# Passes of two gate/up units put side by side, transposes in groups of six and eight, a down unit in 256-column passes

## The chip, the cores and the metric

The kernel runs on one core of a Trainium2 chip. The metric is the device time of one execution in microseconds (us), as the median of several runs. TensorE (PE in the profile) multiplies; its weight loads are listed apart as PEld. VectorE is DVE, ScalarE is ACT, GpSimd is POOL, and SP issues most of the DMAs.

## What is computed

Two layers of a decoder trunk on 256 tokens with model width 1024. The parts that matter here:

```python
for l in range(DEPTH):                                # DEPTH = 2
    x = x + 0.5 * swiglu(rms_norm(x, ffn1_norm[l]), ffn1_gate[l], ffn1_up[l], ffn1_down[l])
    h = rms_norm(x, mix_norm[l]) @ w_in[l]
    # columns of h: pooling | q, k, v of block attention | q, k, v of dilated attention | convolution
    mix = jnp.concatenate([y_pool, y_moba, y_dil, y_conv], axis=-1)
    x = x + mix @ w_out[l]
    x = x + 0.5 * swiglu(rms_norm(x, ffn2_norm[l]), ffn2_gate[l], ffn2_up[l], ffn2_down[l])
return rms_norm(x, final_norm)
# swiglu(x, wg, wu, wd) = (silu(x @ wg) * (x @ wu)) @ wd ; hidden width 2816
```

All weights are float32 in HBM, and each is read once.

## The kernel before

**Weights.** All weights come as units of up to 128 x 2048 columns in a fixed order: for each FFN 22 gate/up units and 16 half down units (two for each of 8 output chunks), for each mixing stage 9 units of w_in and 4 of w_out. A unit lands in two halves (`raw`, four buffers). ACT writes its rounded part `hi` (type fp32r), DVE the rest `lo = raw - hi`; both lie in rings of five units. For three units per mixing stage (the last of w_in, the first two of w_out) ACT writes `lo = -hi` instead and a DMA of POOL adds the raw weights.

**Products.** Activations are split in the same way (`y_f`, `y_m`, `h`, `mx`: hi and lo side by side, 2 x 256 columns). A product is the sum of hi weights times both halves (one pass of 512 columns) and lo weights times the hi half (256 columns). `halves` (line 635) records all 512-column matmuls of a unit, then all 256-column ones, and the other way round at its next call. A gate/up unit has 16 of each, a half down unit 11 of each.

**FFN.** `ffn` (line 688) takes the 22 gate/up units one at a time (the first three of the first FFN together). Each writes two PSUM banks (`mm_gu`); ACT and DVE add up the halves (`t`), scale, apply SiLU and split the result into `h`. Then come the 8 down chunks (`dn`): each is added to `x` by two 256-column DVE operations, and `after(m)` starts the next norm's work on this chunk.

**Mixing stage** (`mix`, line 734). cg and ca (convolution input), then qkd and v (dilated attention), qkm (block attention), pu (pooling), then the output projection wo in the order of `W_OUT`: dilated, pooling, block attention, convolution. Beside these fp32r matmuls stand plain fp32 ones. `rope` (line 812) rotates q and k of each token half and turns them with four 128 x 128 transposes each (`tr_q`, `tr_k`). `scores` gives qk_d and qk_m; `softmax` gives p. `pv` (line 876) turns each head's p with three transposes (`pt`), copies them (`pts`, ACT) and multiplies with v. qk, pv and psw are small matmuls on 64 rows or 64 columns of the array, two at a time. The convolution is a chain of DVE operations on `yv`; then ACT adds the bias to `yv`, and its layer norm (line 936) takes the mean on PE (`ln`, with mean_w), squares (`lsq`), and sums them on PE (`ln` with ones).

**Order.** `Plan.order` (line 169) sets the order of all instructions beforehand: it keeps a clock for each engine, knows a cost for every operation and the buffers that it needs, and gives each engine the ready operation with the earliest due time. PSUM has eight banks: `mm` 0 to 3, `qk` 4 to 6, `sm` 7; gate/up and down units take the oldest of the first seven.

## Time and profile before

| | us |
|---|---|
| median of 3 runs | 936.9 (936.84 to 937.72) |
| profiled execution, device time | 935.79 |
| its span, first to last instruction | 934.0 |
| PE busy | 923.0 |
| DVE busy | 710.9 |
| ACT busy | 573.1 |

The time is that of the whole execution; the span is what the trace covers. A busy PE is a PE with a matmul under way, and matmuls overlap, so the length of a stretch of matmuls is read from the start of the first to the start of what follows, or from the chain of waits, which gives stretches of one kind end to end.

### The profile page before, as it was taken

The numbers are of one execution on the slowest core, as the hardware profiler recorded it, in microseconds if no ns is written. First come the engines' busy times: TensorE is split into PE (matmuls) and PEld (weight loads), VectorE is DVE, ScalarE is ACT, GpSimd is POOL, SyncE is SP. The second block draws the span as 40 slices with busy tenths as digits, with TensorE's granted clock in tenths as the row PEclk, the third lists the DMA queues.
The fourth block names the chain that finished last, engine by engine and source line by source line (L and its number), as shares of the span: only waits on it lengthen the run. The fifth ranks groups of instructions, "written<-read, shape, count | busy, mean of one in ns | idle before, by whom it ended". The sixth has DMA issues, their size and how long they took to land.

```text
span 934.0 us, 14720 instructions
## 1 busy us (share of the span) xinstructions
PE 923.0 (99%) x5460; PEld 813.1 (87%) x5460; DVE 710.9 (76%) x1323; ACT 573.1 (61%) x1055; POOL 44.3 (5%) x57
## 2 busy tenths in 40 slices
PE   9999999999999999999999999999999999999996
PEld 7888888887898888888888888888878988888885
DVE  7899965677978988766778887667698898876652
ACT  7776655558967655554646665445599675665540
POOL 0000000100102000000000000011010200000010
PEclk9999999999999999999999999999999999999998
DMA  8867456662965655456755554567557576554641
GB/s 300 283 215 244 149 155 195 234 217 85 257 207 180 211 195 185 125 177 190 255 199 181 190 187 139 164 193 252 184 125 207 168 249 215 195 168 125 186 125 46
DMA packets 56937, 176.45 MB, mean 189 GB/s; under 512 B 6560, under 2 KB 8608, under 8 KB 56864
## 3 DMA queue, kind: packets, MB, share of 16 engines
q1 hardware_dynamic: 54704, 168.92, 56.0%
q0 software_dynamic: 1728, 6.29, 3.5%
q8 instruction: 43, 0.70, 0.3%
q10 hardware_dynamic: 432, 0.29, 0.1%
q14 instruction: 30, 0.25, 0.1%
HBM read 174.43 MB, written 1.05 MB: 188 GB/s over the span
## 4 chain that ended last, share of the span: by engine, by line
PE 93%; DMA 2%; ACT 2%; DVE 1%; issue 0%; DVEq 0%; SPq 0%; ACTq 0%
PE mm_gu L370 52%; PE dn L370 26%; PE wo L370 3%; PE qkd L370 2%; PE v L370 1%; PE mm_cg L370 1%; PE pu L370 1%; PE mm_ca L370 1%; PE qkm L370 1%; DMA raw<-in_wo_dram 1%; DMA raw<-in_gu_dram 1%; ACT hi L311 1%; DMA x<-in_x_dram 1%; DVE lo L311 0%; PE qk_m L382 0%
## 5 line engine op out<-in xcount | busy, mean ns | idle before, releaser
L311 DVE TENSOR_TENSOR lo<-raw,hi 128x1024 fp32r<-128x1024 f32 (+3 forms) x353 | 374.0, 1083 | 68.5 <-ACT hi L311 52.0
L311 ACT ACTIVATE hi<-raw 128x1024 fp32r<-128x1024 f32 (+3 forms) x365 | 330.8, 939 | 141.9 <-PE dn L370 56.8
L370 PE MATMUL mm_gu<-y_f,hi 128*128 128x512 f32 x1408 | 331.9, 391 | 0.8 <-DVE y_f L348 0.4
L370 PEld LDWEIGHTS mm_gu<-y_f,hi 128*128 128x128 f32 x1408 | 260.5, 188 | 54.4 <-ACT hi L311 1.8
L370 PEld LDWEIGHTS mm_gu<-y_f,lo 128*128 128x128 f32 x1408 | 176.1, 192 | 4.2
L370 PE MATMUL mm_gu<-y_f,lo 128*128 128x256 f32 x1408 | 178.3, 283 | 0.0
L370 PE MATMUL dn<-h,hi 128*128 128x512 f32 x704 | 169.5, 391 | 0.0
L370 PEld LDWEIGHTS dn<-h,hi 128*128 128x128 f32 x704 | 128.8, 188 | 24.0
L311 DVE TENSOR_TENSOR t<-mm_gu,t 128x256 f32<-128x256 f32 x176 | 73.4, 421 | 52.0 <-ACT t L311 48.4
L370 PEld LDWEIGHTS dn<-h,lo 128*128 128x128 f32 x704 | 91.5, 191 | 4.3
L370 PE MATMUL dn<-h,lo 128*128 128x256 f32 x704 | 92.8, 283 | 0.0
L311 ACT ACTIVATE t<-mm_gu 128x256 f32<-128x256 f32 x176 | 64.6, 376 | 37.7 <-PE mm_gu L370 37.6
L311 ACT ACTIVATE h<-th 128x256 fp32r<-128x256 f32 x88 | 36.4, 417 | 63.1 <-DVE th L311 62.9
L311 DVE TENSOR_TENSOR t<-t,rb_f 128x512 f32<-128x512 f32 x88 | 60.2, 687 | 0.9
L311 ACT ACTIVATE th<-t 128x256 f32<-128x256 f32 x88 | 36.2, 414 | 34.9 <-DVE t L311 26.5
L348 DVE SCALAR_TENSOR_TENSOR x<-dn,x 128x256 f32<-128x256 f32 x64 | 27.0, 422 | 38.5 <-PE dn L370 37.9
L370 PE MATMUL wo<-mx,hi 128*128 128x256 f32 x256 | 47.6, 287 | 0.0
L348 DVE SCALAR_TENSOR_TENSOR yv<-hpad,par,yv 128x256 f32<-128x256 f32 x108 | 43.7, 475 | 0.0
L311 DVE TENSOR_TENSOR h<-th,h 128x256 fp32r<-128x256 f32 x88 | 36.9, 420 | 7.8 <-ACT h L311 6.8
L370 PEld LDWEIGHTS wo<-mx,hi 128*128 128x128 f32 x256 | 39.8, 192 | 0.7 <-issue 0.7
L311 DVE TENSOR_TENSOR th<-th,t 128x256 f32<-128x256 f32 x88 | 36.8, 419 | 2.4 <-ACT th L311 1.7
L370 PE MATMUL wo<-mx,lo 128*128 128x256 f32 x128 | 36.2, 283 | 0.0
(198 smaller groups left out, 651.7 us busy)
## 6 DMA issues: line engine op xcount, KB each, us to landing
raw<-in_gu_dram SPq DMA_DIRECT2D x170, 512.0 KB, 4.5
raw<-in_dn_dram SPq DMA_DIRECT2D x64, 384.0 KB, 3.6
raw<-in_dn_dram SPq DMA_DIRECT2D x64, 320.0 KB, 2.9
raw<-in_wi_dram SPq DMA_DIRECT2D x36, 512.0 KB, 4.8
raw<-in_wo_dram SPq DMA_DIRECT2D x16, 512.0 KB, 8.5
lo<-in_wo_dram POOLq DMA_DIRECT2D x8, 512.0 KB, 12.6
raw<-in_gu_dram SPq DMA_DIRECT2D x9, 256.0 KB, 5.7
lo<-in_wi_dram POOLq DMA_DIRECT2D x4, 512.0 KB, 9.4
```

The lines of the kernel that those rows point to most:

```text
L311: f(*[val(x) for x in a], **{n: val(x) for n, x in k.items()})
L348: nc.vector.scalar_tensor_tensor(out, in0=a, scalar=scalar, in1=b, op0=op0, op1=op1)
L370: nc.tensor.matmul(val(o), lhsT=val(lhsT), rhs=val(rhs), start=self.i == 0, stop=self.i == self.n - 1, skip_group_check=True)
```

## The change

Six edits.

- **Pairs.** From the first unit after the norm's row is known (unit 3 in most FFNs, unit 8 in the first one), gate/up units are taken two at a time: all 512-column passes of both, then all 256-column passes of both, and the reverse in the next pair. An odd last unit stays single.
- **Transposes.** `transposes` issues several at once. `rope` turns both token halves together (8 transposes), `pv` two heads together (6).
- **PSUM.** The first of the two pv banks of the dilated attention comes from the `mm` group.
- **Layer norm of the convolution.** One squaring of 512 columns and one addition of 256 columns on DVE, then two sums on PE in place of four.
- **Last down unit.** For the last chunk of the last FFN the first half's two additions to `x` come before the second half, which goes to a bank of its own in 33 passes of 256 columns; one addition follows it.
- **Planner.** A step on PE from fp32 to fp32r or back is charged `TURN` = 0.065; the costs of ACT and of DVE's tensor_tensor per column are raised by 5% and 3%.

```diff
+TURN = 0.065
+        o.kind = any(v.buf.dt == F32R for v in r)
-        out = []
+        out, kind = [], True
-            free[e] = now + o.cost
-            o.done = now + o.cost + o.lat
+            cost = o.cost
+            if e == "pe" and o.kind != kind:
+                cost += TURN
+                kind = o.kind
+            free[e] = now + cost
+            o.done = now + cost + o.lat
...
-        rec("act", 0.093 + 0.000833 * n + 0.093 * extra, nc.scalar.activation, w, [in_, k.get("scale"), k.get("bias")],
+        rec("act", 0.093 + 0.000875 * n + 0.093 * extra, nc.scalar.activation, w, [in_, k.get("scale"), k.get("bias")],
...
-        vec(0.067 + n * 0.001045, name, out, a, b)
+        vec(0.067 + n * 0.00108, name, out, a, b)
...
+    def transposes(items):
+
+        def emit():
+            for o, i in items:
+                nc.tensor.transpose(val(o), val(i), val(ident))
+        plan.op("pe", 0.09 * len(items), emit, w=[o for o, _ in items], r=[i for _, i in items] + [ident])
...
-    def pair_units(nrm, names, blocks=ALL):
+    def pair_units(nrm, names, blocks=ALL, apart=False):
...
+        n = range(len(names))
         for a, b in blocks:
-            i = halves([(s[u][c], ps[u][c], parts[u](2 * k + c), nrm.y[k])
-                        for c in range(2) for k in range(a, b) for u in range(len(names))])
+            order = ([(u, c, k) for u in n for c in range(2) for k in range(a, b)] if apart else
+                     [(u, c, k) for c in range(2) for k in range(a, b) for u in n])
+            i = halves([(s[u][c], ps[u][c], parts[u](2 * k + c), nrm.y[k]) for u, c, k in order])
...
         for f in range(FC):
             nm = f"{l}{w}_{f}"
+            if f > early + 1 and f >= len(ahead) and f + 1 < FC:
+
+                ahead = [None] * f + pair_units(nrm, [f"gu{l}{w}_{f + i}" for i in range(2)], apart=True)
...
+                if nm == f"{DEPTH - 1}1_{KC - 1}" and h == 1:
+
+                    for e in range(2):
+                        stt(T, x[m], ps[:, e * T:(e + 1) * T], 0.5, x[m], ALU.mult, ALU.add)
+                    ps, s = oldest(f"dl{nm}"), Sum()
+                    for i in range(FC // 2):
+                        three(s, ps[:, 0:T], part(i), hh[k0 + i])
+                    stt(T, x[m], ps[:, 0:T], 0.5, x[m], ALU.mult, ALU.add)
+                    after(m)
+                    return th
...
-                for n in range(2):
-                    for c in range(2):
-                        f = n * T + c * 128
-                        transpose(0.09, out[n].on(2 * t + c)[:, c, t * 128:(t + 1) * 128], qk[:, f:f + 128])
+                turned += [(out[n][:, c, t * 128:(t + 1) * 128], qk[:, n * T + c * 128:n * T + c * 128 + 128])
+                           for n in range(2) for c in range(2)]
+            transposes(turned)
...
-            ps = [bank("qk", 2, [128, T], f"pv_{nm}{c}") for c in range(2)]
+            ps = [bank(("mm", "qk")[c] if base == 4 else "qk", 4, [128, T], f"pv_{nm}{c}") for c in range(2)]
...
-        for c in range(2):
-            tt(T, "tensor_mul", sq.on(c)[:, c], yv.on(c)[:, c], yv.on(c)[:, c])
-            for t in range(2):
-                sp.mm(0.15, ps2.on("c")[:, 256 + t:257 + t],
-                      (sq.on(c)[:, c, t * 128:(t + 1) * 128], ones[:, 0:1]))
+        tt(512, "tensor_mul", sq, yv, yv)
+        sq2 = work("acc", 2, [128, T], f"lsq2{l}")
+        tt(T, "tensor_add", sq2, sq[:, 0], sq[:, 1])
+        for t in range(2):
+            sp.mm(0.15, ps2.on("c")[:, 256 + t:257 + t], (sq2[:, t * 128:(t + 1) * 128], ones[:, 0:1]))
```

Since the planner sets the order, the edits move more than they name. Three places, as the built programs have them (names carry layer and number; `hi46` is unit 46's rounded part).

PE in layer 0's mixing stage, from the last pooling matmuls to the first scores of the second head pair, before:

```order
L370 MATMUL pu0_2616<-lo46_2499,y_m0_7_2131 128x256
L370 MATMUL pu0_2616<-hi46_2481,y_m0_7_2131 128x256
L382 MATMUL qk_m00_2739<-km0_2664,qm0_2658 128x128
L382 MATMUL qk_m01_2741<-km0_2664,qm0_2658 128x128
L382 MATMUL qk_m00_2739<-km0_2664,qm0_2658 128x256
L382 MATMUL qk_m01_2741<-km0_2664,qm0_2658 128x256
L370 MATMUL pu0_2616<-hi46_2481,y_m0_7_2131 128x256
L370 MATMUL pu0_2616<-lo46_2499,y_m0_7_2131 128x256
L370 MATMUL pu0_2616<-hi46_2481,y_m0_7_2131 128x256
L370 MATMUL ln0_2752<-yv0_2338,mean_w_72 128x256 x2
L382 MATMUL qk_m02_2763<-km0_2664,qm0_2658 128x128
L382 MATMUL qk_m03_2765<-km0_2664,qm0_2658 128x128
```

The same place on PE now, from the second bank of pv_d on (pooling's last matmul stands right ahead of pv_d):

```order
L389 MATMUL pv_d01_2729<-pts_d03_2713,vt00_2504 64x256
L389 MATMUL pv_d01_2729<-pts_d02_2707,vt01_2510 64x128
L389 MATMUL pv_d01_2729<-pts_d03_2713,vt01_2510 64x128
L389 MATMUL qk_m00_2740<-km0_2660,qm0_2652 128x128
L389 MATMUL qk_m01_2742<-km0_2660,qm0_2652 128x128
L389 MATMUL qk_m00_2740<-km0_2660,qm0_2652 128x256
L389 MATMUL qk_m01_2742<-km0_2660,qm0_2652 128x256
L377 MATMUL ln0_2754<-yv0_2335,mean_w_72 128x256 x2
L389 MATMUL qk_m02_2766<-km0_2660,qm0_2652 128x128
L389 MATMUL qk_m03_2768<-km0_2660,qm0_2652 128x128
L389 MATMUL qk_m02_2766<-km0_2660,qm0_2652 128x256
L389 MATMUL qk_m03_2768<-km0_2660,qm0_2652 128x256
```

Before, 15 pooling matmuls stood after pv_d (12 ahead of qk_m and 3 behind it); now all stand ahead of pv_d, 18 of them ahead of the transposes of q and k, and pv_d, qk_m, ln, qk_m and psw follow each other.

ACT in the same layer, around the bias of `yv` (line 935 before), before:

```order
L311 ACTIVATE hi49_2701<-raw49_0_2549 128x1024
L311 ACTIVATE mx04_2720<-pv_d00_2703 128x256
L311 ACTIVATE mx05_2726<-pv_d01_2708 128x256
L311 ACTIVATE yv0_2338<-yv0_2338,par_322 128x256
L311 ACTIVATE hi49_2701<-raw49_1_2563 128x1024
L311 ACTIVATE yv0_2338<-yv0_2338,par_322 128x256
L311 ACTIVATE ut0_2754<-pu0_2616,y_m0_2224 128x256 x2
```

ACT at that place now:

```order
L318 ACTIVATE hi49_2691<-raw49_1_2562 128x1024
L318 ACTIVATE ut0_2735<-pu0_2600,y_m0_2230 128x256 x2
L318 ACTIVATE mx05_2746<-pv_d01_2729 128x256
L318 ACTIVATE yv0_2335<-yv0_2335,par_311 128x256 x2
L318 ACTIVATE s_m00_2751,dn_m00_2757<-s_m00_2751,mn_m00_2752 128x256
```

The bias still follows the copy of pv_d's second bank, but PE now reaches ln right after pv_d and one pair of scores.

ACT between v and the second rope (unit 46 is the pooling unit, 47 and 48 the first of wo), before:

```order
L311 ACTIVATE vt01_2492<-v01_2368,y_m0_2224 128x512
L311 ACTIVATE lo46_2499<-hi46_2481 128x1024
L311 ACTIVATE hi46_2481<-raw46_1_2287 128x1024
L311 ACTIVATE lo46_2499<-hi46_2481 128x1024
L311 ACTIVATE hi47_2527<-raw47_0_2308 128x1024
L311 ACTIVATE hi47_2527<-raw47_1_2323 128x1024
L311 ACTIVATE lo47_2546<-hi47_2527 128x1024 x2
L311 ACTIVATE qkmt00_2574<-qkm00_2488,qc0_2246 128x256
L311 ACTIVATE qkmt00_2574<-qkm00_2488,y_m0_2224 128x256
L311 ACTIVATE hi48_2582<-raw48_0_2506 128x1024
L311 ACTIVATE hi48_2582<-raw48_1_2529 128x1024
L311 ACTIVATE qkmt01_2603<-qkm01_2516,qc0_2246 128x256
```

ACT now, where unit 46 stands (ahead of the dilated softmax):

```order
L318 ACTIVATE gt03_2379<-hpad_84,par_311 128x256 x2
L318 ACTIVATE hi46_2385<-raw46_0_2244 128x1024
L318 ACTIVATE hi46_2385<-raw46_1_2273 128x1024
L318 ACT_TABLE_LOAD
L318 ACTIVATE s_d00_2398,dn_d00_2408<-s_d00_2398,mn_d00_2399 128x256
L318 ACTIVATE s_d01_2402,dn_d01_2420<-s_d01_2402,mn_d01_2403 128x256
L318 ACTIVATE s_d00_2398,dn_d00_2408<-s_d00_2398,mn_d00_2399 128x128
L318 ACTIVATE s_d01_2402,dn_d01_2420<-s_d01_2402,mn_d01_2403 128x128
L318 ACTIVATE lo46_2434<-hi46_2385 128x1024
L318 ACTIVATE p_d00_2452<-s_d00_2398,rd_d00_2437 128x256
L318 ACTIVATE p_d01_2456<-s_d01_2402,rd_d01_2442 128x256
```

The rounding of unit 46 moved ahead of the softmax, and with it the moment at which the raw buffers of unit 48 come free; layer 1 has the same order with units 135 and 137.

## Rows read from the trace of the kernel before

**Rows 1.** Page, part 1: busy time, share of the span, instructions.

```profile
PE 923.0 (99%) x5460; PEld 813.1 (87%) x5460; DVE 710.9 (76%) x1323; ACT 573.1 (61%) x1055; POOL 44.3 (5%) x57
```

**Rows 2.** Chain of waits, whole span: start us, length us, engine, tile, line, matmuls.

```profile
298.45 105.58 PE mm_gu L370 x608
...
739.27 11.36 PE mm_gu L370 x64
```

**Rows 3.** Timeline of PE, gate/up: start, length, line, what, count.

```profile
301.93 4.00 PE L370 MATMUL mm_gu<-y_f,lo 128*128 128x256 f32 x32
305.76 7.44 PE L370 MATMUL mm_gu<-y_f,hi 128*128 128x512 f32 x32
313.05 4.00 PE L370 MATMUL mm_gu<-y_f,lo 128*128 128x256 f32 x32
```

**Rows 4.** Chain of waits, layer 0, v between the two rope transposes.

```profile
214.16 2.07 PE v L370 x9
```

**Rows 5.** Chain of waits, layer 0, from the second attention's transposes to wo.

```profile
242.71 0.66 PE pt_d L311 x6
...
244.79 1.45 PE pv_d L382 x16
246.24 1.63 PE pu L370 x12
...
252.07 1.26 PE wo L370 x9
253.34 0.13 PE ln L370 x2
...
254.44 0.33 PE pt_m L311 x3
254.77 0.56 PE ln L370 x6
255.33 1.18 PE wo L370 x9
```

**Rows 6.** Chain of waits, layer 1, the DMA of unit 137's second half.

```profile
689.25 7.84 DMA raw<-in_wo_dram
```

**Rows 7.** Timeline of PE, layer 1, at the second group of pt_d.

```profile
698.60 0.28 PE L370 MATMUL pu<-hi,y_m 128*128 128x256 f32 x1
699.34 0.55 PE L311 MATMUL pt_d<-ident,p_d 128*128 128x128 f32 x3 [0.46 <-ACT pts_d L311]
```

**Rows 8.** Chain of waits, layer 0: the first transpose after qkm.

```profile
238.60 0.29 PE tr_qm L311 x2
```

**Rows 9.** Timeline of DVE, layer 0: the last step of the second rope.

```profile
240.43 0.29 DVE L311 TENSOR_TENSOR qkmt<-ra_m,rb_m 128x128 f32<-128x128 f32 x1
```

**Rows 10.** Timeline of ACT, layer 0: copy of pv_d's second bank, bias of yv.

```profile
246.29 0.38 ACT L311 ACTIVATE mx<-pv_d 128x256 fp32r<-128x256 f32 x1 [0.27 <-PE pv_d L382]
246.69 0.51 ACT L311 ACTIVATE yv<-yv,par 128x256 f32<-128x256 f32 x1
```

**Rows 11.** Timeline of PE, start of the second FFN of layer 0.

```profile
280.05 0.63 PE L370 MATMUL mm_gu<-y_f,hi 128*128 128x512 f32 x2
281.09 1.84 PE L370 MATMUL mm_gu<-y_f,hi 128*128 128x512 f32 x6 [0.41 <-DVE y_f L348]
282.77 0.51 PE L370 MATMUL mm_gu<-y_f,lo 128*128 128x256 f32 x3
```

**Rows 12.** Chain of waits, layer 0, from the last pt_m to that start.

```profile
260.24 0.95 ACT hi L311
...
270.66 6.85 DMA raw<-in_gu_dram
...
277.60 1.06 ACT hi L311
278.65 0.41 ACT y_f L311
```

**Rows 13.** Chain of waits, after the last matmul of the last down chunk.

```profile
923.67 0.44 DVE x L348
...
924.13 0.43 DVE x L348
```

**Rows 14.** Who waited for whom, whole span: us in total, times, longest.

```profile
ACT hi L311 <- PE dn L370: 56.8, 36, 3.2
...
ACT hi L311 <- PE mm_gu L370: 23.4, 23, 1.4
```

**Rows 15.** Busy time by stretch, layer 0: PE, PEld, DVE, ACT, POOL, PEclk, DMA share, GB/s.

```profile
239.00:262.00 23.00, 23.00 (x203) 20.32 (x200) 18.29 (x64) 20.63 (x51) 1.73 (x2) 1.00 0.89 234
```

More of the change, by code (lines that the diff above doesn't have):

```diff
@@ L60, with __init__ @@
 class Buf:
-    def __init__(self, make, before):
+    def __init__(self, make, before, dt=None):
+        self.dt = dt
         self.make, self.before, self.tile, self.whole = make, before, None, False
@@ L108 @@
 class Op:
-    __slots__ = ("eng", "cost", "emit", "deps", "after", "wait", "late", "done", "lat", "lead")
+    __slots__ = ("eng", "cost", "emit", "deps", "after", "wait", "late", "done", "lat", "lead", "kind")
 class Plan:
@@ L118, in buf @@
         last = self.places.get(key)
-        b = Buf(lambda: pool.tile(shape, dt, tag=tag, name=name), last.users if last else [])
+        b = Buf(lambda: pool.tile(shape, dt, tag=tag, name=name), last.users if last else [], dt)
         self.places[key] = b
@@ L815, in rope @@
             out = [bank("qk", 2, [128, 2, T], f"tr_{n}{nm}{l}") for n in "qk"]
+            turned = []
             for t in range(2):
@@ L878, in pv @@
             st = []
-            for h in range(4):
-                pt = bank("qk", 2, [128, 384], f"pt_{nm}{h}")
-                for j in range(3):
-                    s = slice(j * 128, (j + 1) * 128)
-                    transpose(0.09, pt.on(j)[:, s], p[h].on(min(j, 1))[:, s])
-                st.append(flat(slot(place + h, f"pts_{nm}{h}"))[:, 0:384])
-                A(384, st[h], pt, AF.Copy)
-            ps = [bank("qk", 2, [128, T], f"pv_{nm}{c}") for c in range(2)]
+            for hs in ((0, 1), (2, 3)):
+                pts = [bank("qk", 2, [128, 384], f"pt_{nm}{h}") for h in hs]
+                s = [slice(j * 128, (j + 1) * 128) for j in range(3)]
+                transposes([(pt[:, s[j]], p[h].on(min(j, 1))[:, s[j]]) for pt, h in zip(pts, hs) for j in range(3)])
+                for pt, h in zip(pts, hs):
+                    st.append(flat(slot(place + h, f"pts_{nm}{h}"))[:, 0:384])
+                    A(384, st[h], pt, AF.Copy)
+            ps = [bank(("mm", "qk")[c] if base == 4 else "qk", 4, [128, T], f"pv_{nm}{c}") for c in range(2)]
             items = []
```

## The prediction

> **What bounds the kernel now.** I read the page's table of engines first. PE is busy for 923.0 of a span of 934.0 us, DVE for 710.9 and ACT for 573.1 [rows 1]: an edit is worth what it takes from PE's own stretches or from the few gaps between them. The chain of waits shows the same from the other side. It runs along PE nearly everywhere, and in a whole FFN it is one piece: 19 gate/up units, 608 matmuls, 105.58 us without a hole, 5.557 us each [rows 2]. So I next need the price of one matmul in a plain run, from the timeline, start to start. In gate/up 32 matmuls of 256 columns stand from 301.93 to 305.76, 3.83 or 0.120 each, and 32 of 512 columns from there to 313.05, 7.29 or 0.228 each [rows 3]. (The lengths in the rows, 4.00 and 7.44, hold the modelled end of the last one, which lies beside the next.) These stretches already hold the change from one kind to the other, and a unit at these prices is 16 x 0.228 + 16 x 0.120 = 5.56: the whole of it. The kernel can gain only in the mixing stages, at the FFN starts and at the end.
>
> **Pairs.** They halve the changes between 512 and 256 columns in gate/up. A change is no longer than what the rows leave unexplained: nine 512-column matmuls of v, which have a change at either end, take 2.07 [rows 4], 0.230 each where gate/up has 0.228, so 0.02 for two changes. There are some 40 changes in the four FFNs, half go: at most 20 x 0.02 = 0.4, at least 0. I take 0.0075 for each, **-0.15**, since gate/up itself shows no trace of them.
>
> **Transposes.** Two edits. Where they stand among 512-column matmuls, a group should hide less: nine matmuls of v with a group on either side take those 2.07 against 9 x 0.228 = 2.05, 0.02 for a group. Among 256-column matmuls six transposes in a row take 0.66 and three take 0.33 [rows 5]: 0.11 each in either case, so six together cost what two threes cost. Fewer groups save 0.02 to 0.1 per layer; I take 0.05.
>
> **fp32 among fp32r.** Here is the largest term. Twelve pooling matmuls behind pv_d take 1.63, while 12 x 0.120 = 1.44; nine of wo behind a pair of ln sums take 1.26 and 1.18 against 1.08 [rows 5]. So coming back from a small fp32 group costs 0.10 to 0.19. In the new order pv_d, qk_m, ln, qk_m and psw follow each other: two returns fewer, between 0.1 (one, at the smaller price) and 0.37; I take 0.3, since the pooling row is the one that these groups stood beside. Half the sums of the layer norm: `ln x6` at 0.56 and `ln x2` at 0.13 become half, 0.35, with 0.05 to 0.1 of a return: 0.4 per layer. The DVE price of this edit (one operation of 512 columns and an addition for two of 256) lies beside other work. With the transposes that is **-0.8 per layer** on PE, bounds -0.5 and -1.0 (from 0.02 + 0.1 + 0.35 to 0.1 + 0.37 + 0.5).
>
> The row shows a loss at each return to fp32r. The Trainium skill ("TensorEngine Tiling (Array Packing)", Key Properties) has another account: "Changing tiling mode (not just tile) drains the TensorE". Then the 64-column pv, the 64-row qk and the full-array ln would still pay at each border inside the new block, one change of seven would go, and the total below would be about 0.3 us higher. The rows have no two such groups side by side, so they don't decide it.
>
> **A wait that goes.** In layer 1, PE stands before the second group of pt_d: the pooling matmul ends near 698.73 and the transposes start at 699.34, 0.61 later. ACT, which must copy the group ahead, is in `hi` of unit 137, and this waits for its second half, which took 7.84 us from 689.25 on [rows 6, 7]. Now unit 135's rounding stands ahead of the softmax, and the raw buffer for unit 137 comes free earlier by the whole of the softmax on ACT, a dozen operations. I count **-0.65**; at worst half of it stays, as another transfer ends late.
>
> **Waits that come.** The eight transposes of the second rope need both token halves. PE's first transposes of it start at 238.60 [rows 8]; the last DVE step of the second half ends at 240.43 + 0.29 = 240.72, 2.1 to 2.4 behind the end of qkm [rows 9]. PE has 18 pooling matmuls to put in between, 18 x 0.120 = 2.16. That leaves 0 to 0.5; I take +0.2. Behind this wait on PE stand pt_d and the rest of pooling. Second, PE reaches the mean of the layer norm right behind pv_d and one pair of scores, about 1.45 + 0.86 = 2.3 after pv_d's start. On ACT the copy of pv_d's second bank starts 1.50 after that start, and two bias operations follow, to 2.9 [rows 10]. PE waits 0 to 0.6 there, with qk_m's second pair and psw behind it, and softmax behind these; I take +0.25. So a mixing stage ends, on PE, -0.8 + 0.45 = -0.35 earlier in layer 0 and -0.8 - 0.65 + 0.45 = **-1.0** in layer 1.
>
> **What is late next: the FFN behind it.** In layer 0 its first eight 512-column passes take from 280.05 to 282.77, 2.72 instead of 8 x 0.228 = 1.82 [rows 11]. The chain ahead is ACT's: `y_f` stands behind a `hi` that waited for a DMA of 6.85, and ahead of that stands the convolution's layer norm [rows 12]. In layer 1 the same start costs little: two units take 11.36 against 2 x 5.557 = 11.11 [rows 2], because that FFN starts with 256-column passes, which need only the rounded half of `y_f`. Now the kinds are swapped: layer 0 starts with the 256-column passes, layer 1 with the others. Layer 0 then keeps its 0.35 and wins about half of its 0.9: **-0.8**. Layer 1 now pays the 0.9 where it paid 0.25, and its chain of ACT and DMA, which ends no earlier for a faster PE, takes back another 0.2: it keeps **-0.15** of 1.0. If the swap costs nothing, layer 1 keeps all of it; that is the first rival.
>
> **The last down unit.** Two additions to `x` stand at the end, 0.44 and 0.43 with the second starting at 924.13 [rows 13]; now one does: -0.46 (924.13 - 923.67). 33 passes of 256 columns, 33 x 0.120 = 3.96, take the place of 11 x (0.228 + 0.120) = 3.83: +0.13. Together **-0.33**.
>
> **What hides the rest.** DVE is busy for 76% and ACT for 61% of the span [rows 1], and ACT in `hi` waited for PE for 56.8 us at dn and 23.4 at gate/up [rows 14]: the rings are full, and a pair that holds two of five places still leaves three ahead. I cost this at nothing; without that cover each pair could add up to a pass of one unit, 1.9 us. The clock stood at 1.00 over a stretch with twenty transposes and PE busy for 23.00 of 23.00 [rows 15], its upper level of 2.4 GHz; I cost it at nothing.
>
> **Sum.** -0.15 - 0.8 - 0.15 - 0.33 = -1.43. The profiled execution took 935.79, so 934.4 in its terms; the median shown is 1.1 above it, 936.9, and 936.9 - 1.4 = **935.5**.
>
> **The rivals.**
> *(A) The swap of kinds costs nothing.* The chain of ACT and DMA at the FFN starts moves with PE, so the mixing stages' gain stays: -0.15 - 0.8 - 1.0 - 0.33 is -2.3, and with both new waits at half their size -2.7: **934.2**. For it: the wait for the DMA there is set by a buffer that comes free with PE's own progress [rows 12]. Against it: layer 0's 0.9 in the present order [rows 11].
> *(B) The starts take everything.* y_f comes at the same time whatever PE does, so only the pairs and the end count, -0.48: **936.4**. For it: the chain ahead of the start is not PE's for some 18 us [rows 12].
> *(C) Slower: the softmax of block attention loses its cover.* Fifteen pooling matmuls, 15 x 0.120 = 1.8 us and 0.4 for two returns, stood between pv_d and pt_m; from 244.79 to 254.44 PE had 9.65 us of work while ACT and DVE made the probabilities [rows 5]. Now PE has some 7.4 us there. If the others still need the whole 9.65, PE waits 2.2 in each layer. The starts behind then lose nothing more to ACT, so 4.4 stands on top of (A)'s -2.3: +2.1, **939.0**. It decides from 0.7 us per layer on, where the forecast's 1.4 is gone. For it: pt_m cannot start before the softmax ends. Against it: ACT starts on the scores as soon as qk_m ends, which the same fifteen matmuls no longer delay, and wo's dilated half can fill.
> *(D) The clock falls.* If the longer runs of transposes and small matmuls let the clock drop to 1.2 GHz, 7 us of work per layer would take 14: about **950**. Against it: the row at 1.00 [rows 15]. The Trainium skill ("TensorE: Matmul & The Clock Gate", Part 4) says that the full clock doesn't engage for transposes; the trace does not agree, with 1.00 over twenty of them.
>
> **How the numbers follow.** Forecast 0.50, A 0.27, B 0.13, C 0.09, D 0.01. About 0.2%, 1.9 us, is what a measurement of this kernel can tell from no change: below 935.0 is faster, above 938.8 slower. A is nearly all faster (0.25), and of the forecast's own spread of 0.7 about a fifth (0.10): 0.35. C and D are slower: 0.10. The rest, 0.55, is within. The range runs from 933.9, A with a little more, to 937.6, B with the upper bounds of the new waits, and leaves out C and D and the low end of A.
>
> **What the profile after would show.** The piece of 19 gate/up units in the chain at 105.4 to 105.6 [rows 2]. PE matmuls at 5463. No gap at pt_d in layer 1 [rows 7]; gaps of 0.1 to 0.5 at the eight transposes and at ln. The start of the second FFN of layer 0 with at most 0.5 over its plain price, that of layer 1 with about 0.9. One addition behind the last matmul [rows 13]. I am wrong if pt_m waits for ACT by over 1 us, if wo is broken by waits that it did not have, or if units wait for `hi` or `lo` in gate/up.

## The result and the profile after

The changed kernel takes 932.12 us (932.06 to 932.32), the kernel before 936.87 in the runs beside it: 0.9948 of it, 95% interval 0.9932 to 0.9964. The forecast of 935.5 was too high, and the range, from 933.9, did not hold the time. The four runs of before that stand in this ratio (936.1 to 937.7) turned out to be high ones: in the runs beside the experiments below before had medians of 935.22 to 935.65, and the changed kernel, run beside it twice more, was 0.9967 (0.9955 to 0.9978) and 0.9964 (0.9951 to 0.9978) of it, 3.05 and 3.17 us faster. The profiled executions say the same: their spans are 934.0 and 930.5, so 3.5 less.

Page, part 1, of the changed kernel (compare [rows 1]): 3.1 us less of PE with three more matmuls.

```profile
PE 919.9 (99%) x5463; PEld 812.8 (87%) x5463; DVE 706.3 (76%) x1324; ACT 574.5 (62%) x1055; POOL 46.3 (5%) x57
```

Chain of waits, changed kernel, layer 0, from pooling to the second FFN (start, length, what; answers to [rows 5, 8, 12]):

```profile
238.67 2.16 PE pu L377 x18
240.83 0.22 PE tr_qm L401 x2
...
245.15 1.43 PE pu L377 x12
246.59 1.45 PE pv_d L389 x16
248.04 0.85 PE qk_m L389 x8
248.89 0.02 issue
248.91 1.13 PE ln L377 x4
...
251.98 1.26 PE wo L377 x9
...
262.91 16.74 PE wo L377 x138
279.64 11.15 PE mm_gu L377 x64
290.79 0.34 PE st_f L377 x4
...
297.04 105.49 PE mm_gu L377 x608
```

Before, this chain left PE after the last pt_m and ran over ACT, DVE and a DMA for over 18 us [rows 12]; now it stays on PE. The eight transposes at 240.83 follow the pooling matmuls with no gap. The same chain in layer 1, where PE stood for 0.61 [rows 6, 7], and the end of the kernel [rows 13]:

```profile
698.41 1.07 PE pu L377 x9
699.48 0.66 PE pt_d L401 x6
...
736.35 11.15 PE mm_gu L377 x64
...
916.57 3.97 PE dl L377 x33
920.54 0.02 issue
920.57 0.44 DVE x L355
921.00 0.02 issue
```

Timeline of ACT, changed kernel, layer 0 (start, length, operation, idle before it and what ended that):

```profile
258.50 1.06 ACT L318 ACTIVATE hi<-raw 128x1024 fp32r<-128x1024 f32 x1
259.58 0.87 ACT L318 ACTIVATE pts_m<-pt_m 128x384 f32<-128x384 f32 x2
260.34 1.06 ACT L318 ACTIVATE hi<-raw 128x1024 fp32r<-128x1024 f32 x1
...
275.59 1.06 ACT L318 ACTIVATE hi<-raw 128x1024 fp32r<-128x1024 f32 x1 [1.41 <-DMA raw<-in_gu_dram]
276.55 0.89 ACT L318 ACTIVATE y_f<-x,gain 128x256 fp32r<-128x256 f32 x2
```

The same in the kernel before:

```profile
259.75 0.49 ACT L311 ACTIVATE pts_m<-pt_m 128x384 f32<-128x384 f32 x1 [0.56 <-PE pt_m L311]
260.14 2.00 ACT L311 ACTIVATE hi<-raw 128x1024 fp32r<-128x1024 f32 x2
...
277.60 1.06 ACT L311 ACTIVATE hi<-raw 128x1024 fp32r<-128x1024 f32 x1 [3.14 <-DMA raw<-in_gu_dram]
278.56 0.90 ACT L311 ACTIVATE y_f<-x,gain 128x256 fp32r<-128x256 f32 x2
```

A rounding stands now ahead of the last two copies of pt_m, at 258.50; before, the first came behind them, at 260.14. y_f stands behind another `hi` that waits for a DMA, and starts at 276.55 where it started at 278.56. Timeline of SP, the issue of that DMA, before and now:

```profile
270.66 0.33 SPq L311 DMA_DIRECT2D raw<-in_gu_dram  x1
```

```profile
269.74 0.33 SPq L318 DMA_DIRECT2D raw<-in_gu_dram  x1
```

Counted from qkm's first matmul (227.56 before, 227.63 now) the transfer goes at 43.1 before and at 42.1 now, and y_f starts at 51.0 and at 48.9. So about half of the 2.1 us is an earlier issue. The other half is the transfer itself, which took 6.85 before and 5.77 in this execution.

So the 3.5 us of the spans divide like this. Between qkm's first matmul and the second FFN's first one, PE takes 51.85 in each layer, where it took 52.48 and 53.18: -0.63 and -1.33. From there to the norm's sums (`st_f`) it takes 11.15 twice, where it took 12.03 and 11.36: -0.88 and -0.21. (These four are distances between starts in PE's timeline.) The pieces of 19 gate/up units are 0.09 to 0.1 shorter [rows 2], some 0.35 in four FFNs, and the end 0.34. That is 3.7; the norm's sums of the first FFN came 0.2 later in this execution (45.97 against 45.80 in the chains).

### The profile page after: what moved, and what is told of

It reads as the page before. It is cut to its first block, busy times and chain, and to the rows that moved or that the text cites. A ratio compares the mean times of both kernels' runs of the same rounds, so it can differ in the third digit from the quotient of the medians.

```text
span 930.5 us, 14715 instructions
## 1 busy us (share of the span) xinstructions
PE 919.9 (99%) x5463; PEld 812.8 (87%) x5463; DVE 706.3 (76%) x1324; ACT 574.5 (62%) x1055; POOL 46.3 (5%) x57
## 4 chain that ended last, share of the span: by engine, by line
PE 98%; DMA 1%; DVE 0%; ACT 0%; issue 0%; DVEq 0%; ACTq 0%
PE mm_gu L377 52%; PE dn L377 26%; PE wo L377 5%; PE v L377 2%; PE qkd L377 2%; PE qkm L377 2%; PE pu L377 1%; PE mm_cg L377 1%; PE mm_ca L377 1%; DMA raw<-in_gu_dram 0%; PE dl L377 0%; PE qk_d L389 0%; PE qk_m L389 0%; PE ln L377 0%; PE pv_d L389 0%; PE pv_m L389 0%
## 5 line engine op out<-in xcount | busy, mean ns | idle before, releaser
L318 DVE TENSOR_TENSOR lo<-raw,hi 128x1024 fp32r<-128x1024 f32 (+3 forms) x353 | 371.9, 1079 | 66.6 <-ACT hi L318 43.1
L377 PE MATMUL mm_gu<-y_f,hi 128*128 128x512 f32 x1408 | 327.4, 390 | 0.5 <-ACT hi L318 0.4
L377 PEld LDWEIGHTS mm_gu<-y_f,lo 128*128 128x128 f32 x1408 | 173.9, 192 | 3.6 <-DVE lo L318 1.0
L377 PE MATMUL mm_gu<-y_f,lo 128*128 128x256 f32 x1408 | 175.7, 283 | 0.7 <-DVE lo L318 0.7
L377 PE MATMUL dn<-h,hi 128*128 128x512 f32 x693 | 166.8, 390 | 0.0
L377 PEld LDWEIGHTS dn<-h,hi 128*128 128x128 f32 x693 | 126.7, 188 | 23.7
L318 ACT ACTIVATE h<-th 128x256 fp32r<-128x256 f32 x88 | 36.3, 414 | 44.2 <-DVE th L318 44.1
```

What stands on the lines that cost most here:

```text
L318: f(*[val(x) for x in a], **{n: val(x) for n, x in k.items()})
L377: nc.tensor.matmul(val(o), lhsT=val(lhsT), rhs=val(rhs), start=self.i == 0, stop=self.i == self.n - 1, skip_group_check=True)
```

## The experiments

All kernels of this table ran with one profile each, timed beside before on the same chip. "Mixing" is PE's time from qkm's first matmul to the second FFN's first, "start" from there to `st_f` (11.15 is a start without a loss), layer 0 and layer 1, read from PE's timeline of the profiled execution. The last column is the median against before's in the runs beside it. The 95% interval of the ratios is about 0.8 us to either side for kernels near before and up to 1.2 for the fastest ones, so e3, g1, g2 and g3 can't be told from no change, and e1 and i1 only just.

| kernel | mixing 0, 1 | start 0, 1 | against before |
|---|---|---|---|
| before | 52.48, 53.18 | 12.03, 11.36 | |
| changed | 51.85, 51.85 | 11.15, 11.15 | |
| e1 pairs alone | 52.48, 53.47 | 11.65, 11.20 | -0.46 |
| e2 groups alone | 52.40, 52.40 | 11.47, 11.15 | -1.31 |
| e3 layer norm alone | 52.00, 52.75 | 11.79, 12.62 | +0.52 |
| e4 planner alone | 54.13, 54.66 | 12.06, 12.33 | +4.55 |
| f1 changed, again | 51.85, 51.86 | 11.67, 11.61 | -3.05 |
| f2 changed, old costs | 52.00, 52.00 | 11.15, 11.17 | -3.24 |
| f3 changed, no groups | 53.61, 53.79 | 11.97, 12.54 | +1.74 |
| f4 groups and costs | 52.25, 52.26 | 11.17, 11.15 | -1.56 |
| g1 y_f first | 53.31, 52.89 | 11.43, 11.16 | +0.08 |
| g2 five raw buffers | 52.52, 52.50 | 12.07, 11.64 | +0.83 |
| g3 pt_m's groups alone | 53.17, 52.98 | 11.18, 11.15 | -0.18 |
| g4 changed, g1 and g2 | 51.86, 51.87 | 11.15, 11.15 | -3.29 |
| h1 changed, old layer norm | 52.26, 52.26 | 11.15, 11.45 | -2.22 |
| h2 changed, no pairs | 51.86, 51.86 | 11.45, 11.15 | -2.74 |
| h3 changed, third time | 51.84, 51.84 | 11.24, 11.83 | -3.17 |
| h4 as g4, again | 51.85, 51.85 | 11.15, 11.16 | -4.08 |
| i1 ropes' and pt_d's groups | 52.42, 52.41 | 12.13, 12.73 | +0.97 |
| i2 as g4, ln mean later | 51.92, 51.88 | 11.15, 11.16 | -3.15 |

**Which part does it.** Theory 1: y_f of the second FFN is late because of an order on ACT, and the groups of transposes change it. Rivals: the swap of kinds by the pairs (theory 2), the planner's costs (theory 3).

```diff
...
+            if f > early + 1 and f >= len(ahead) and f + 1 < FC:
+
+                ahead = [None] * f + pair_units(nrm, [f"gu{l}{w}_{f + i}" for i in range(2)], apart=True)
```

> The kernel before with the pairs of gate/up units alone. The pairs swap the kinds of pass with which the second FFNs start (layer 0 now with 256 columns, layer 1 with 512), all else in the mixing stages stays. Theory 1 (what cleared the FFN starts is an earlier y_f, which stands on ACT behind the rounding of a gate/up unit, and that rounding behind a transfer that was issued earlier): without the edits of the mixing stage y_f comes as late as before, so the starts keep most of what they lost, layer 0 between 0.4 and 1.4 us, layer 1 between 0.2 and 1.2; gate/up pieces of 19 units go from 105.58 to 105.49; in all -0.3 to -0.8 us. Theory 2 (the swap of kinds itself clears the starts): layer 0 loses nothing, layer 1 nothing, in all -1.5. The prediction's step: layer 0 about -0.45, layer 1 about +0.85 at the start, in all about +0.1.

935.19 against 935.65 (0.9991, 0.9982 to 1.0). Starts of 11.65 and 11.20: with the kinds swapped and nothing else, layer 0 lost less and layer 1 did not lose more. The sum fits theory 1 in size. Layer 0 is a clean test of the swap: y_f starts 1.5 us ahead of PE's first gate/up matmul, as before, and the start loses 0.50 where it lost 0.88. Layer 1 is none: there y_f starts 3.3 ahead, where it was 1.8 before, since the transfer took 5.1 us for 6.5. So the 0.85 that the prediction charged to layer 1 is not tested here.

```diff
...
+            transposes(turned)
...
+                transposes([(pt[:, s[j]], p[h].on(min(j, 1))[:, s[j]]) for pt, h in zip(pts, hs) for j in range(3)])
...
+            ps = [bank(("mm", "qk")[c] if base == 4 else "qk", 4, [128, T], f"pv_{nm}{c}") for c in range(2)]
```

> The kernel before with the transposes in groups of eight and six and the PSUM bank of pv_d alone. Theory 1 (grouping frees ACT earlier for the rounding of the units ahead of y_f): the 512-column start of layer 0 loses at most 0.2 us instead of 0.9, layer 1 at most 0.1 instead of 0.25, y_f starts 1.5 us or more earlier than before, and with the wait of 0.61 at pt_d gone and two returns to fp32r fewer per layer the whole is -2 to -2.6 us. Theory 2 (the swap of kinds): the starts lose what they lost, 0.9 and 0.25, the whole is -0.9 to -1.3. Theory 3 (the planner's new costs moved the rounding): y_f as late as before, pt_d's wait stays, the whole is -0.3 to -0.6.

934.34, -1.31 (0.9986, 0.9977 to 0.9995), less than theory 1 wanted, but its signs are there: no wait at pt_d, 52.40 in both layers, and starts of 11.47 and 11.15 without any swap. What was wrong is PE's own share: two returns fewer bring 0.08, not 0.3.

```diff
...
+        tt(512, "tensor_mul", sq, yv, yv)
...
+        tt(T, "tensor_add", sq2, sq[:, 0], sq[:, 1])
...
+            sp.mm(0.15, ps2.on("c")[:, 256 + t:257 + t], (sq2[:, t * 128:(t + 1) * 128], ones[:, 0:1]))
```

> The kernel before with the layer norm's sums halved alone (one squaring of 512 columns, one addition, two sums on PE for four). By the prediction's term 0.4 us per layer of PE time. Theory 1: the gain in layer 0 is lost again at the FFN start, whose y_f is still late (start loss 0.9 to 1.3), layer 1 keeps it: -0.4 to -0.8 in all. Theory 2 the same. A theory in which the layer norm's shorter chain brings y_f forward: the start of layer 0 loses under 0.4, in all -1.3 or more.

936.17, +0.52 (1.0003, 0.9994 to 1.0012), no change that can be told. PE's stretch is 0.48 and 0.43 shorter, as expected. Layer 0 kept it (the start is 11.79, before 12.03), and layer 1's start gave it back and more (12.62): its transfer ahead of y_f goes 43.7 us after qkm's first matmul, before 43.8, so y_f did not come with PE. Both layers came out the other way round from what was expected.

```diff
+TURN = 0.065
...
-        rec("act", 0.093 + 0.000833 * n + 0.093 * extra, nc.scalar.activation, w, [in_, k.get("scale"), k.get("bias")],
+        rec("act", 0.093 + 0.000875 * n + 0.093 * extra, nc.scalar.activation, w, [in_, k.get("scale"), k.get("bias")],
...
-        vec(0.067 + n * 0.001045, name, out, a, b)
+        vec(0.067 + n * 0.00108, name, out, a, b)
```

> The kernel before with the planner's new costs alone (a step between fp32 and fp32r charged 0.065, ACT and DVE dearer by 5% and 3% per column). Theory 1: other orders, the same transfers: within 0.5 us of before, the waits at pt_d in layer 1 and at the FFN start of layer 0 still there. Theory 3 (the costs moved the rounding of units 46, 50, 135 and 139 forward and with it the transfers): pt_d's wait gone, the start of layer 0 at most 0.3, in all -1.2 or more.

940.20, +4.55 (1.0048, 1.0036 to 1.0061): all theories missed. Chain of waits of this kernel, layer 0:

```profile
238.29 12.25 DMA raw<-in_wo_dram
250.54 0.02 issue
250.56 1.06 ACT hi L318
251.62 0.73 ACT ut L318 x2
252.35 1.76 ACT s_m L318 x8
```

The new costs put a rounding of a wo unit ahead of the softmax of block attention on ACT; its transfer takes 12.25 us, and PE runs out of work that doesn't need s_m. It is what rival (C) feared, a softmax that PE waits for, but reached by a rounding ahead of it and not by pooling matmuls that are gone.

**Do the costs matter in the change, and do the groups?** f1 is the changed kernel itself; f2 takes the costs back, f3 the groups, f4 has just these two.

> The changed kernel as it is, timed beside the kernel before on the same chip, since the runs of before spread over 3 us. If the spread of before is a spread of its waits for DMAs (first loads, the rounding ahead of pt_d in layer 1, the starts of the second FFNs), the changed kernel, which has none of the last three, keeps to within 0.5 us over all its runs, and the difference of the medians is 3 to 4 us, as the spans of the profiled runs say (930.5 against 934.0), not the 4.75 of the first four runs.

932.59 (932.52 to 933.42) beside 935.64 (933.64 to 938.04): a spread of 0.9 (6 runs) against 4.4. The profiled execution was the slowest of its six and lost 0.5 at both starts, so the changed kernel is not free of that loss in every run. Timeline of SP and of ACT, layer 0:

```profile
270.19 0.33 SPq L318 DMA_DIRECT2D raw<-in_gu_dram  x1
```

```profile
277.52 1.06 ACT L318 ACTIVATE hi<-raw 128x1024 fp32r<-128x1024 f32 x1 [3.34 <-DMA raw<-in_gu_dram]
278.49 0.90 ACT L318 ACTIVATE y_f<-x,gain 128x256 fp32r<-128x256 f32 x2
```

The transfer goes at the same point as in the first profile, 42.1 us after qkm's first matmul, but it took 7.25 us for 5.77, and y_f starts 1.5 ahead of PE for 2.9.

```diff
-TURN = 0.065
...
-            if e == "pe" and o.kind != kind:
```

> The changed kernel with the planner's old costs (no TURN, ACT and DVE as before). Theory 1 (the groups of transposes clear the waits, the costs only follow the traces): PE's stretch from pu to the second FFN within 0.4 us of the changed kernel's 51.85 in each layer, FFN starts 11.15 to 11.5, in all 0 to +0.8 against the changed kernel. Theory 3 (the gain is an order that only the new costs give, together with the groups): a wait at pt_d, at the layer norm's mean or at an FFN start returns, +1 or more.

932.40, 0.2 from f1: the new costs are worth nothing measurable here. In this order, as in g3 below, y_f stands ahead of the rounding that waits for the transfer; it starts 3.7 us ahead of PE.

```diff
-            transposes(turned)
...
+                        transpose(0.09, out[n].on(2 * t + c)[:, c, t * 128:(t + 1) * 128], qk[:, f:f + 128])
...
+                    transpose(0.09, pt.on(j)[:, s], p[h].on(min(j, 1))[:, s])
```

> The changed kernel with the transposes one by one again and both pv banks of one group: pairs, halved layer norm sums, last down unit and the planner's new costs stay. The new costs alone made the kernel before 4.6 us slower, by a rounding of a wo unit that stands on ACT ahead of the softmax of block attention and waits 12 us for its transfer. Theory 1 (that order belongs to the single transposes): it is there again, +1.5 to +4 against before, +5 to +8 against the changed kernel. Theory 4 (it belongs to the old layer norm or to the unpaired units): the time is within 1 us of before less 0.34 for the last unit, 0.5 to 1 for the layer norm.

937.38, +1.74 against before, +4.8 against f1, at the low end of theory 1 and just under it. The 12 us transfer ahead of the softmax is back (238.22 12.23 in its chain), and both starts lose.

```diff
+TURN = 0.065
...
+            transposes(turned)
```

> The kernel before with the groups of transposes and the planner's new costs, nothing else. The groups alone were -1.2 to -1.8, the costs alone +4.6. Theory 1 (the groups take away what the costs stumble over): -1.5 to -2.5, PE's stretch from qkm's end to the second FFN at 52.0 to 52.4, no wait for ACT longer than 0.3 in it. Theory 5 (the two add up): +3.

934.08, -1.56 (0.9986, 0.9977 to 0.9995): theory 1. They don't add up; the groups leave the costs nothing to stumble over.

**Is it y_f, and the transfer ahead of it?**

```diff
+LATER = {54: "f01", 143: "f11"}
...
+            first[self.name] = len(plan.ops) - 1
...
+            plan.hold = first.get(LATER.get(n)) if i == 0 else None
```

> The kernel before with one dependency more: the rounding of the first half of units 54 and 143 on ACT comes behind the rounding of y_f for the second FFN, where it stood ahead of it. PE's order is the same to the instruction. Theory 1 (y_f is late only because it stands behind a rounding that waits for its transfer): from the first gate/up matmul of the second FFN to the norm's sums 11.15 to 11.3 us in both layers (12.03 and 11.36 in the profile of before), in all -0.8 to -1.2 us; the wait of about 0.6 at pt_d in layer 1 stays. Rival (the start is bound by DVE's part of y_f or by the additions to x): 11.7 or more in layer 0, in all less than -0.4.

Timeline of ACT, layer 0 of this kernel:

```profile
274.70 1.06 ACT L312 ACTIVATE hi<-raw 128x1024 fp32r<-128x1024 f32 x1 [1.80 <-DMA raw<-in_gu_dram]
277.39 0.92 ACT L312 ACTIVATE y_f<-x,gain 128x256 fp32r<-128x256 f32 x2 [1.63 <-DVE x L312]
```

y_f waits for nothing but `x`, and the starts are 11.43 and 11.16, close to what was expected. Yet the median is 935.30 beside 935.22: in this execution the wait at pt_d was in layer 0 as well (0.8; a transfer of 7.97 us), and no second profile of before tells how much its starts vary. The starts of this profile bear the mechanism out, the -0.8 to -1.2 was not shown.

```diff
-RAW, RING = 4, 5
+RAW, RING = 5, 5
...
-                a = work("ra", 2, [128, 8, 16], f"ra_{nm}{l}{t}")
-                b = work("rb", 2, [128, 8, 16], f"rb_{nm}{l}{t}")
+                a = work("ra", 1, [128, 8, 16], f"ra_{nm}{l}{t}")
+                b = work("rb", 1, [128, 8, 16], f"rb_{nm}{l}{t}")
```

> The kernel before with five raw buffers instead of four (two small buffers of the rope given up for the place). PE's order is the same. Theory 1 (the waits are for transfers that were issued late, since no raw buffer was free): the wait at pt_d in layer 1 goes, the starts of the second FFNs lose under 0.3, in all -1.2 to -2.2 us, and the runs spread over 1 us or less instead of 3 to 4. Rival (the transfers are slow at these places because the DMA engines are full, whenever they are issued): in all 0 to -0.5, spread as before.

936.05, +0.83. Half of it came: with a fifth buffer no wait is left at pt_d (52.52 and 52.50). But the starts lose as before. In the order on ACT the planner used the buffer to put both halves of unit 54 ahead of y_f instead of one, so y_f stood behind a later transfer; that one took 5.6 us, and y_f starts 2.8 us ahead of PE in layer 0, more than the 1.5 of before. What loses the 0.92 is the order on DVE, as in i1 below.

```profile
276.94 1.06 ACT L311 ACTIVATE hi<-raw 128x1024 fp32r<-128x1024 f32 x1 [0.88 <-DMA raw<-in_gu_dram]
277.90 0.90 ACT L311 ACTIVATE y_f<-x,gain 128x256 fp32r<-128x256 f32 x2
```

**Which group clears which wait.** g3 and i1 are the two halves of e2.

```diff
+            for hs in ((0, 1), (2, 3)) if base != 4 else ((0,), (1,), (2,), (3,)):
```

> The kernel before with only the transposes of block attention's p (pt_m) in groups of six; those of the two ropes and of the dilated attention stay single. Theory 1 (the groups of pt_m free ACT for a unit's rounding, which brings the transfers ahead of y_f forward): starts of the second FFNs at 11.15 to 11.4, PE's stretch from pu to the second FFN shorter by 0 to 0.3, the wait at pt_d in layer 1 stays: -0.8 to -1.4. Rival (the other groups, in the ropes and pt_d, do it by a shorter or earlier softmax): the starts lose what they lost, 0 to -0.4.

Starts of 11.18 and 11.15, clean as expected; the wait at pt_d stays in both layers, 0.73 and 0.54, and by that much PE's stretch is longer than before's 52.48 without one. 935.04, -0.18: the sum is not theory 1's, since this kernel waited at pt_d twice. Nor is the mechanism quite: no rounding moved ahead of the last pts_m here, and the transfer that y_f stood behind goes no earlier (44.2 us after qkm's first matmul in layer 0, the wait at pt_d included; 43.1 before). The planner put y_f ahead of the rounding that waits, as g1 did by hand, and y_f starts 3.7 ahead of PE in both layers.

```diff
+            transposes(turned)
...
+            for hs in ((0, 1), (2, 3)) if base == 4 else ((0,), (1,), (2,), (3,)):
```

> The kernel before with the transposes of the ropes in groups of eight and of pt_d in groups of six; pt_m stays single. Theory 1 (each group clears its own wait): no wait for ACT at pt_d in either layer, PE's stretch from qkm's start to pv_d the same in both layers (19.0 to 19.2 with the first rounds of pu in it); the starts of the second FFNs still lose 0.3 to 1 in layer 0; -0.4 to -1.0 in all. Rival (pt_m's groups do all): the wait stays in one layer or both, 0 to -0.3.

No wait at pt_d, and the starts lose 0.98 and 1.58. Chain of waits, layer 0:

```profile
259.74 0.49 ACT pts_m L311
260.24 0.95 ACT hi L311
...
270.65 5.99 DMA raw<-in_gu_dram
...
276.72 1.06 ACT hi L311
277.78 0.41 ACT y_f L311
278.19 0.03 issue
278.21 0.49 DVE y_f L348
278.70 0.67 DVE x L311 x2
279.37 1.27 DVE y_f L348 x2
280.64 0.67 DVE x L311 x2
281.31 0.60 DVE y_f L348
```

This is [rows 12] again, to 0.01 us up to the transfer: the rounding after the last pts_m, and everything behind it. So the groups of the ropes and pt_d clear pt_d, and those of pt_m clear the starts. 936.59, +0.97, where -0.4 to -1.0 was expected. Layer 1's start takes back all of the 0.8 that its mixing stage won. But y_f's first chunk is not the cause by itself: the transfer is 0.9 shorter than before, and y_f starts 2.7 us ahead of PE (280.40), where it was 1.5 before. Behind it the order on DVE is another one. The additions to `x` for the third and fourth chunk stand behind the first y_f there (278.70), before they stood ahead of it (277.37 in DVE's timeline), so the later chunks of y_f come late all the same. e4 and g2 have this order too, with y_f 2.6 to 2.8 ahead, and lose 0.5 to 1.2.

**What the other parts are worth in the changed kernel.**

```diff
+                      (sq.on(c)[:, c, t * 128:(t + 1) * 128], ones[:, 0:1]))
```

> The changed kernel with the layer norm's old four sums on PE. In the changed kernel the starts of the second FFNs have y_f in time, so PE time counts in full. Theory 1: two sums more per layer, 0.35, and their border, 0.1: PE's stretch from pu to the second FFN at 52.3 instead of 51.85, starts as in the changed kernel, +0.8 to +1.1 us. Rival (the layer norm's later end makes y_f late again): starts lose 0.5 or more in addition, +1.5 to +2.5. Rival (the sums stood beside waits): 0 to +0.3.

933.41 against h3's 932.46, +0.95: 0.41 per layer of PE is 0.82 of it. Theory 1 to the number.

```diff
-            if f > early + 1 and f >= len(ahead) and f + 1 < FC:
```

> The changed kernel with single gate/up units, which also gives layer 0's second FFN its start with 512 columns back and layer 1's its start with 256. Theory 1 (the swap costs nothing, pairs are worth 0.1 per FFN): starts at 11.15 to 11.5 in both layers, pieces of 19 units at 105.6 instead of 105.5, +0.3 to +0.5 us. The prediction's step (layer 0's 512-column start loses half of 0.9 or more, layer 1's 256-column start 0.25 or less): layer 0 at 11.6 to 12.1, layer 1 at 11.15 to 11.4, about -0.2.

932.89, +0.43 against h3. The pieces of 19 units go back up by 0.1, and the starts, with the kinds as before, are 11.45 and 11.15, with y_f 2.6 us ahead of PE in both. That is theory 1: the starts are nearly clean without the swap. (The runs of h2 and h3 overlap.)

> The changed kernel, beside h4 on one chip: 932.1 to 932.7, -2.7 to -3.6 against before.

932.46, as expected. For the starts in layer 1, see the table: 0.68 lost in this execution.

**A faster version.** g4 and h4 put g1 and g2 into the changed kernel, with both halves of units 54 and 143 held:

```diff
-RAW, RING = 4, 5
+RAW, RING = 5, 5
...
+            plan.hold = first.get(LATER.get(n))
```

> The changed kernel with both: five raw buffers, and the rounding of units 54 and 143 behind y_f. PE's order is the changed kernel's. Theory 1: the changed kernel loses at the two starts only 0 to 0.5 each and nothing at pt_d, and its first loads wait; so -0.2 to -1.0 against the changed kernel, about 931.5 to 932.3, with all runs within 0.5. Rival (nothing is left there, the rest is PE's own time): within 0.2.

> The changed kernel with five raw buffers and y_f ahead of the rounding of units 54 and 143, beside h3 on one chip. Theory 1 (the changed kernel still loses 0 to 0.5 at each start in some runs): 0.2 to 0.6 under h3. Rival: within 0.15 of it.

931.93 (931.80 to 932.34), then 931.55 (931.35 to 932.75) beside h3's 932.46 (932.11 to 932.82). Against before 0.9960 and 0.9959 (0.9946 to 0.9971). No start loses anything in either profile. y_f starts 3.7 us ahead of PE in all four. The median is 0.9 lower than the changed kernel's on the same chip, though the runs of the two overlap.

```diff
+        pooled = len(plan.ops) - 1
...
+        plan.hold = pooled
```

> The changed kernel with five raw buffers, y_f first, and the mean of the layer norm held until the pooling's psw has been issued, so that it no longer stands between the two pairs of scores of block attention. The planner puts six matmuls of wo there in its place. If each border between kinds of small matmuls costs 0.1 and the wait for the bias 0.1: PE's stretch from pv_d to pv_m 14.6 to 14.8 instead of 14.88, 0 to -0.5 in all against the version with five raw buffers (931.6 to 931.9). If the later layer norm makes y_f late: starts lose, +0.3 or more.

932.47. From pv_d to pv_m it is 14.21 instead of 14.87, as hoped, and from there to the FFN 18.83 instead of 18.09: the planner gave six matmuls of wo the place between the scores, with two borders of their own. Nothing won.

## Why the prediction was wrong

- **The starts (the step that failed).** The prediction took the chain of ACT and DMA ahead of y_f as unmoved ("ends no earlier for a faster PE") and let the swap of kinds decide: layer 0 wins half of 0.9, layer 1 pays 0.9 where it paid 0.25. In the profile both starts are clean: -0.88 and -0.21 against -0.45 and +0.85, 1.5 of the 2.3 us by which the parts of the profile (-3.7) miss the sum of -1.43. Of the rest 0.6 is the mixing stages' and 0.2 the pairs'. What decides is how far y_f comes ahead of PE. With single pt_m groups and y_f in its old place (before, e1, e3, e4, f3, i1) the starts lose 0.79 and 0.98 on average; with grouped ones (changed, e2, f1, f2, f4, g3, h1, h2, h3) 0.14 and 0.16. (In e4 and i1 the order on DVE adds to the loss.) The groups act by the order on ACT: in the changed kernel a rounding moved ahead of the last pts_m, and the transfer ahead of y_f goes 42.1 us after qkm's first matmul in both layers of all three profiles, where it went at 43.1 and 43.8. PE's stretch is 0.63 and 1.33 shorter, so y_f gains 0.35 on PE in each. In f2 and g3 y_f stands ahead of the rounding itself. That new order was there to be read in the new program, and it was not weighed.
- **What was luck.** In layer 0 of the first profile y_f is 2.9 us ahead of PE, before 1.5. Of these 1.4 only 0.35 are the order; 1.1 are a short transfer (5.8 us, before 6.9). In f1 and h3, the same kernel, it took 7.3 and 6.8, and y_f came hardly earlier against PE than before, 1.5 and 1.9 ahead. Over its three profiles the changed kernel loses 0.20 and 0.38 at the starts, 0.5 less than the one profile of before, where +0.4 was forecast. By that average the starts are 0.9 of a miss of some 1.7 us (medians -3.05 and -3.17). Before has one profile only, so its own average stays open.
- **The swap of kinds** has the sign and nearly the size that was said, at a late y_f: 1.5 us ahead of PE, a 512-column start loses 0.88 (before) and a 256-column start 0.50 and 0.52 (e1, f1, layer 0); 1.8 to 1.9 ahead, 0.46 (f1, layer 1) against 0.21 and 0.09 (before, layer 1; h3, layer 0). Among the grouped kernels a 512-column start loses 0.24 on average, a 256-column start 0.07.
- **Rival (A)** was near in the starts' sum (-0.45 against -0.5 on average), with a reason that does not hold: in e3 PE is 0.4 to 0.5 earlier and the transfer at most 0.1. It moves with the order on ACT. In layer 1 of e3 and i1, where PE came 0.4 and 0.8 earlier, the start took it all and more: there **rival (B)** is what happens.
- **The wait at pt_d:** right, and for the reason given. The transfer that ACT waited for was issued at 689.25 [rows 6]; the same one, the fourth half of w_out's units, goes at 677.73 now, by the timeline of SP. That the wait comes in layer 0 too in kernels whose edit leaves this place alone (g1, g3) was not seen.
- **Waits that come.** The eight transposes waited 0 in both layers, not 0.2: 18 pooling matmuls just cover the rope. At the mean of the layer norm 0.29 was lost (1.13 and 0.02 against 0.86), near the 0.25, but only some 0.08 can be a wait for ACT: ln starts 0.39 behind the last qk_m, and 0.31 in e2. The rest lies inside ln, whose second matmul starts 0.33 behind the first (0.32 in e2), where it took 0.21 before.
- **fp32 among fp32r.** Two returns to pooling did go (1.63 for 12 [rows 5] became 1.43, 0.55 for 3 became 0.36), 0.39 in all, but the mean between the scores costs 0.29. Net 0.08 in layer 0 (e2), not 0.3. The Trainium skill ("TensorEngine Tiling (Array Packing)", Key Properties) says that a change of tiling mode drains TensorE; the trace agrees so far as `ln` with 64-row scores on both sides takes 1.13, and 0.86 with them on one side. The halved sums are worth 0.41 per layer (h1), as predicted.
- **The pairs** are worth some 0.35 in the profile and 0.4 in the medians (h2), near the upper bound, not 0.15: 105.49 to 105.50 against 105.58 to 105.60 for 19 units.
- **The last down unit:** -0.34 in the profile (61.30 for 61.22 from dn's start to the end, and 6.30 for 6.72 behind it) against -0.33.
- **(C)** did not come in the changed kernel; e4 shows another way to a late softmax. **(D)** did not come: from 239 to 263 us, with the groups of eight and six in it, the granted clock is 1.00, the upper of the two levels (below).
- **The base.** 1.2 to 1.7 us of the first difference of 4.75 lie in which runs of before were at hand, and the prediction started from three of them.

Busy time by stretch, changed kernel, layer 0 (stretch, length, PE, PEld, DVE, ACT, POOL, PEclk, DMA share, GB/s; answers to [rows 15]):

```profile
239.00:263.00 24.00, 23.98 (x211) 21.34 (x210) 20.99 (x67) 21.22 (x54) 1.73 (x2) 1.00 0.76 202
```

## What to carry to other kernels

Where an engine works in a fixed order, look for what a late operand stands behind, not for what it needs: y_f needed only `x`, and waited for a rounding, which waited for a transfer, which waited for a buffer. A gain ahead of such a point can be lost there (layer 1 of e3 and i1), so price an edit together with the waits behind it. The halved layer norm and the groups of ropes and pt_d gained nothing alone (+0.5 and +1.0, the first within noise); in the changed kernel the layer norm is worth 0.95 (h1), and all groups together gain 1.3 (e2). And take more than one profile of a kernel that waits for a transfer: its length alone moved these starts by half a microsecond.

## What was not expected of the hardware

- Transfers of one size vary: 512 KB for `raw` took 6.0, 6.9, 7.8 and 12.3 us from issue to landing in these chains, and from 5.8 to 7.3 at one place of one kernel (changed, f1). Before waits for such transfers and its runs spread over up to 4.4 us; f2, whose starts wait for none, spread over 0.4, though with 5 runs only, so that the one causes the other is not shown.
- A border between kinds of small matmuls costs about 0.1 also inside a block of fp32 ones: the second matmul of ln starts 0.32 to 0.33 behind the first where ln follows 64-row scores (changed, e2), and 0.21 where it follows pooling (before).
